# Second feed-forward, last eight tiles: the down projection by seven block products, with half of the weight sums made earlier on GpSimd

## The chip, the cores and the metric

The kernel runs on one core of one Trainium2 chip. Five engines share the work: TensorE (PE) multiplies matrices, VectorE (DVE) and ScalarE (ACT) do elementwise work and move results out of PSUM, GpSimd (POOL) does elementwise work in SBUF, and SyncE (SP) issues the transfers. The metric is the time of one execution on the device in microseconds (us), as the median of several runs.

## The reference

One layer on 512 latent tokens and 256 context tokens, all in float32, with model width 1024:

```python
def ffn_sublayer(h_in, shift, scale, gate, norm_w, w1, w3, w2):
    h = modulate(rms_norm(h_in, norm_w), shift, scale)
    return h_in + 0.5 * gate * swiglu(h, w1, w3, w2)      # swiglu: (silu(h @ w1) * (h @ w3)) @ w2
...
    x = ffn_sublayer(x, mx[0], mx[1], mx[2], norm1_w, ffn1_w1, ffn1_w3, ffn1_w2)
    ctx = ffn_sublayer(ctx, mc[0], mc[1], mc[2], norm1_w, ffn1_w1, ffn1_w3, ffn1_w2)
    proj = modulate(rms_norm(x, norm2_w), mx[3], mx[4]) @ w_in
...
    x = x + mx[5] * token_mix(proj, k_all, v_all, rope, ...)
...
    x = ffn_sublayer(x, mx[6], mx[7], mx[8], norm3_w, ffn2_w1, ffn2_w3, ffn2_w2)
    return x
```

`w1` and `w3` are 1024 x 2816 and `w2` is 2816 x 1024. The inner width 2816 is handled as 22 tiles of 128, `f` = 0 to 21. The first feed-forward runs on latent and context tokens, the second on the latent tokens alone. Only the latent stream is returned.

## The kernel before

**Precision.** A float32 product is made of three passes over operands that are split into a high and a low part: high x high, low x high, high x low (`mm3`). ScalarE casts the high part (`oph`) and VectorE subtracts it from the source for the low part (`opl`). In the trace these are `CAST oph<-raw` or `oph<-block`, and `TENSOR_TENSOR opl<-raw,oph` or `opl<-block,oph`.

**Up projections.** From f=4 on (the first four tiles are plain) both feed-forwards form `h @ w1` and `h @ w3` of a tile together by the seven-product scheme of Strassen and Winograd: halves of the model dimension, the two weight matrices, and two halves of the tokens are the 2x2 blocks. `Winograd.unit` (L938) issues seven products, named B11, T1, B21, T2, T3, T4 and B22 after their token-side block; in the second feed-forward each is 12 matmuls of 128x256. The weight side needs four sums of the four 512-column quarters of a weight block of 1 MB; `prep` and `wants` (L851, L861) have GpSimd make them (`s<-block`, three times `block<-...`), 128x512 each. VectorE combines the results out of PSUM and writes the gated tile as a split pair `gh`, `gl`.

**Down projection.** After some units, `down_flow` (L791) multiplies the finished tiles of a chunk with their rows of `w2`: 8 output tiles x n tiles x 3 passes of 128x512, each output tile added to `x` with the gate. `CHUNKS2 = [4, 4, 4, 4, 2, 4]` sets the chunks; the last of them, f=18 to 21, is done by `down` behind the units, with the output transfers in its evacuations (`ev3` L2298 and `ev_half`).

**What sets the order.** Instructions that go through the recording helper stand at L60 in the profile and keep the order in which they are written, on their engine. `Flow` (`slot`, L105) runs ahead of PE: it prepares operand pairs in the order of a list (`plan`, L894), five pairs ahead, up to nine during a down; `product` (L912) takes one pair each and lets the number shrink back by one per unit. Semaphore waits between engines follow from the data.

**End of the first feed-forward.** Its last chunk of six tiles (f=16 to 21) goes down in two halves of 384 tokens: `last_mm` (L1227) is called 16 times, 8 output tiles for group 0 and then 8 for group 1. `last_ev` (L1238) adds a result to `x` on VectorE and squares it on ScalarE; `SsqAcc` (L414) sums the squares on VectorE (`sqa`), and the total goes as a split pair `sqh`, `sql` through PE (`mm<-sql,ones`). `norm2` (L1244) then makes the normalised tokens of the group (`hf`, and the pair `hh`, `hl`). The normalisation of group 0 runs on VectorE beside the down part of group 1, and that of group 1 beside the input projection (`in_k`, L1317), in which the matmuls with `ones` stand at a fixed place. GpSimd has no work there.

Of the kernel before, what the change touches and what calls it, by code (L numbers as in the profile page):

```python
# [31 lines left out]
CHUNKS2 = [4, 4, 4, 4, 2, 4]  # L32
# [43 lines left out]
class Halves:  # L76
# [5 lines left out]
    def __getitem__(self, key):  # L82
        i = key[1].start // 512
        return self.tiles[i][:, key[1].start - 512 * i : key[1].stop - 512 * i]

# [96 lines left out]
def layer_kernel(ctx: ExitStack, tc: tile.TileContext, xT, wfirst, wst, wada, wuq, wkpe, cols, wrope, vnw, rope, out):  # L182
# [4 lines left out]
    const = ctx.enter_context(tc.tile_pool(name="const", bufs=1))  # L187
    raws = ctx.enter_context(tc.tile_pool(name="raws", bufs=RAWS))
# [636 lines left out]
    U_DN2 = U_UP2 + 44  # L825
# [13 lines left out]
    class Winograd:  # L839


        def __init__(self, pool, n, u0, blocks, g_tile, sl_bufs, s1_bufs, third=None, held=None):
            self.third, self.held = third, held
            self.sl_bufs, self.s1_bufs = sl_bufs, s1_bufs
            self.ready = (None,)
            self.pool, self.n, self.u0, self.blocks, self.g_tile = pool, n, u0, blocks, g_tile

        def tmp(self, name, n, bufs=1):
            return self.pool.tile([P, n], F32, tag=name, bufs=bufs, name=f"{name}_{nc.next_id()}")

        def prep(self, f, eng=None, early=False):  # L851
            r = st.block(wst, (self.u0 + 2 * f) // 2, self.third if f % 3 == 0 else None)
            q = [r[:, i * 512 : i * 512 + 512] for i in range(4)]
            s1 = self.tmp("s1", 512, self.s1_bufs)
            if f != self.held:
                (eng or nc.gpsimd).tensor_add(s1, q[2], q[3])
            if early:
                eng.tensor_sub(q[2], q[0], q[2])
            self.ready = f, q, s1, nc.gpsimd if early else eng or nc.gpsimd, early

        def wants(self, f):  # L861
            q, s1, eng = [], [], []
# [9 lines left out]

            def block_sums():
# [12 lines left out]
            def third():  # L886
                a = st.operand(q[1])
                eng[0].tensor_sub(q[1], q[1], q[0])
                return a
# [4 lines left out]
        def plan(self, flow, f0, downs, late=False):  # L894
# [4 lines left out]
            for f in range(f0, NF):  # L899
                nxt = self.wants(f + 1) if f + 1 < NF else None  # L900
                nx = nxt[:1] if nxt else ()
                if f == self.late:
                    flow.todo.extend((w[3], w[4], w[2]) + nx + (w[1],) + w[5:])
                elif nxt is None:
# [7 lines left out]
        def product(self, bank, blk, first, pend, step=None, cut=False):  # L912
# [4 lines left out]
            flow.slot(step or (lambda: None))  # L917
            prod(bank, a, self.blocks[blk], self.n, first, cut)
# [3 lines left out]
        def open(self, f, step, f0=None, splits=()):  # L922
# [12 lines left out]
            self.product(banks[0], "B11", True, evac(), step)  # L935
            return banks, p1

        def unit(self, f, hd, step):  # L938
# [10 lines left out]

            def ev_u2():  # L950
# [3 lines left out]
            def ev_u2z():  # L954
                v.tensor_add(u2, Y, p1)
                yield
                v.tensor_add(Z, Z, u2)

            def ev_u3():
                nc.scalar.copy(u3, W)  # L960
                v.tensor_add(u3, Z, u3)
                yield

            def ev_lo():
                v.tensor_add(W, W, u2)
# [4 lines left out]
            def ev_hi(seeded=False):  # L970
# [4 lines left out]
                v.tensor_mul(Z, Z, u3)  # L975
# [11 lines left out]
            if f == self.late or f + 1 == NF:  # L987
# [11 lines left out]
            seeded = f != self.late and f + 1 < NF  # L999
            if f + 1 < NF and nxt is None:  # L1000
                nxt = self.open(f + 1, None)
            self.product(banks[3], "T4", False, ev_lo(), lambda: step(f, 3))
            self.product(banks[2], "B22", False, ev_hi(seeded), cut=n > 256 and f in DOWN1)
            return nxt

        def run(self, flow, f0, after, step=lambda f, i: None, opening=None, splits=()):
# [3 lines left out]
            for f in range(f0, NF):  # L1010
                hd = self.unit(f, hd, step)
                after(self.flow, f)
            flow.slot()
            other_banks()

# [210 lines left out]

    def last_mm(g, dt, mid=lambda: None):  # L1227
        pt = mm()
# [65 lines left out]
    for dt in range(NK):  # L1294
# [14 lines left out]
        pt = last_mm(1, dt, lambda: next(hA) if dt == 1 else None)  # L1309
    fctx.close()  # L1310
# [836 lines left out]
    def g2_tile(f):  # L2147
        gt[f] = tuple(f2.tile([P, 512], F32R, tag=t, bufs=6, name=f"{t}_{nc.next_id()}") for t in ("gh", "gl"))
# [51 lines left out]
    def diffs(i, j, between):  # L2200
# [23 lines left out]
    def ends2(f):  # L2224
        return [ci for ci in range(len(CHUNKS2) - 1) if starts2[ci] + CHUNKS2[ci] == f]

# [45 lines left out]
    wino = Winograd(f2, 256, U_UP2, blocks, g2_tile, 2, 2, f2, NPLAIN2 + 1)  # L2272
# [25 lines left out]
    def ev3(pt, dt, g, gn):  # L2298
        evac_lat(pt, dt, 2)
        nc.sync.dma_start(two(out[:, dt, :]), lat(x, dt))  # L2300

    def ev_half(pt, dt, g, gn):
        evac_x(pt, dt, seg_of(g // 256)[:1], 2)
        o = slice(g // 256 * 384, g // 256 * 384 + 256)
        nc.sync.dma_start(out[:, dt, g : g + 256], x[:, dt, o])

# [5 lines left out]
    st.more = f2ctx.enter_context(tc.tile_pool(name="ops2", bufs=1)), MORE  # L2312
    wino.run(flow, NPLAIN2, after2, splits=splits)
# [106 lines left out]
```

## Time and profile before

| | |
|---|---|
| median of 3 runs | 1104.12 us (1104.03 to 1104.24) |
| the profiled execution | 1104.5 us |
| its span (first to last instruction) | 1102.5 us |
| first feed-forward's last down, group 0 and group 1 | about 490 to 516 and 516 to 541 us |
| second feed-forward's units (from f=4) and downs | about 797 to 1100 us |
| granted TensorE clock, mean | 1.00 |
| moved from and to HBM | 122.58 and 2.10 MB |

Times in the profile are microseconds, "busy" is the time in which an engine executed, and the share is that of the span. A row of the trace has start, duration, engine, line of the kernel, operation, result and inputs by name, and the shape; a bracket behind it gives the engine's idle time just before and what ended it. A row of a group has the count, the busy time and the mean of one in ns, and the idle time before such instructions. "PEld" is TensorE's weight load, which runs beside the matmuls.

### The profile page before, as it was taken

To read this page: it belongs to the slowest core of one execution; us is meant where nothing else is said; L and a number is where in the kernel's file an instruction comes from. 1 tells how busy PE (TensorE), PEld (TensorE's weight loads), DVE (VectorE), ACT (ScalarE), POOL (GpSimd) and SP (SyncE) were. 2 spreads that over 40 slices of the span, in tenths; PEclk is the share of its full clock that TensorE was granted. 3 is DMA by queue.
4 is the path that set the end of the run, shared out by engine and by line. 5 is a ranking of instruction groups with operands and counts; after the bars stand their busy time and mean duration, and the time that the engine had idled before them with its cause. 6 is when DMAs were issued, how large, how long until landed. Compare 5 with 4: busy or idle time off the path is not lost.

```text
span 1102.5 us, 19621 instructions
## 1 busy us (share of the span) xinstructions
PE 1097.5 (100%) x7610; PEld 1052.5 (95%) x7610; DVE 892.8 (81%) x1594; ACT 536.5 (49%) x1115; POOL 310.3 (28%) x269
## 2 busy tenths in 40 slices
PE   9999999999999999999999999999999999999998
PEld 7899999999999999999998889999999989898997
DVE  5779998888878769866867899989988878787883
ACT  6545422431344214443765549986663535354450
POOL 0003303311344013400009317860014444352420
PEclk9999999999999999999999999999999999999999
DMA  9721354234334664412241310103222322424202
GB/s 354 279 60 47 120 172 139 100 137 148 106 124 151 233 201 164 149 54 93 97 132 61 102 50 21 39 21 102 91 94 89 123 78 93 137 78 132 99 21 77
DMA packets 35677, 125.95 MB, mean 114 GB/s; under 512 B 3712, under 2 KB 10624, under 8 KB 30976
## 3 DMA queue, kind: packets, MB, share of 16 engines
q1 hardware_dynamic: 35440, 124.63, 33.2%
q8 instruction: 60, 0.98, 0.4%
q14 instruction: 33, 0.27, 0.1%
q10 hardware_dynamic: 144, 0.06, 0.1%
HBM read 122.58 MB, written 2.10 MB: 113 GB/s over the span
## 4 chain that ended last, share of the span: by engine, by line
PE 96%; DMA 1%; DVE 1%; ACT 1%; POOL 0%; issue 0%; SPq 0%; ACTq 0%; POOLq 0%; DVEq 0%
PE mm L60 61%; PE one L60 20%; PE big L60 10%; PE big L616 1%; PE mm L601 1%; DMA scale<-wada 1%; PE mm L177 1%; PE mm L176 1%; PE mm L178 1%; PE mm L338 1%; DMA x<-xT 0%; PE big L608 0%; DVE sq L60 0%; POOL pe L60 0%; ACT hh L60 0%
## 5 line engine op out<-in xcount | busy, mean ns | idle before, releaser
L60 DVE TENSOR_TENSOR opl<-block,oph 128x512 fp32r<-128x512 f32 x216 | 195.4, 912 | 32.6 <-ACT oph L60 29.9
L60 POOL TENSOR_TENSOR block<-block 128x512 f32<-128x512 f32 x69 | 105.0, 1522 | 378.9 <-DVE opl L60 376.2
L60 ACT CAST oph<-block 128x512 fp32r<-128x512 f32 x216 | 132.3, 622 | 108.8 <-PE mm L60 85.5
L60 PE MATMUL mm<-gl,oph 128*128 128x256 f32 (+2 forms) x573 | 176.4, 308 | 0.0
L60 PE MATMUL mm<-gh,opl 128*128 128x256 f32 (+2 forms) x573 | 176.4, 308 | 0.0
L60 PE MATMUL mm<-gh,oph 128*128 128x256 f32 (+2 forms) x573 | 176.4, 308 | 0.0
L60 PEld LDWEIGHTS mm<-gh,oph 128*128 128x128 f32 x573 | 107.6, 188 | 5.5
L60 PEld LDWEIGHTS mm<-gh,opl 128*128 128x128 f32 x573 | 107.6, 188 | 5.4
L60 PEld LDWEIGHTS mm<-gl,oph 128*128 128x128 f32 x573 | 107.6, 188 | 5.4
L60 ACT CAST oph<-raw 128x512 fp32r<-128x512 f32 x127 | 76.0, 620 | 69.7 <-PE mm L60 44.4
L60 DVE SCALAR_TENSOR_TENSOR x<-mm,g,x 128x512 f32<-128x512 f32 (+2 forms) x136 | 78.7, 600 | 28.5 <-PE mm L60 27.9
L60 DVE TENSOR_TENSOR opl<-raw,oph 128x512 fp32r<-128x512 f32 x127 | 88.1, 710 | 15.3 <-ACT oph L60 14.0
L60 POOL TENSOR_TENSOR block<-s,block 128x512 f32<-128x512 f32 x35 | 48.3, 1379 | 123.8 <-DVE opl L60 122.3
L60 PE MATMUL mm<-hh,oph 128*128 128x384 f32 (+2 forms) x195 | 64.9, 333 | 0.0
L60 PE MATMUL mm<-hl,oph 128*128 128x384 f32 (+2 forms) x195 | 64.8, 333 | 0.0
L60 PE MATMUL mm<-hh,opl 128*128 128x384 f32 (+2 forms) x195 | 64.8, 333 | 0.0
L60 DVE SCALAR_TENSOR_TENSOR junk<-raw,cb 128x1024 bf16<-128x1024 f32 x48 | 62.1, 1308 | 0.2 <-DMA raw<-wada 0.2
L60 POOL TENSOR_TENSOR s<-block 128x512 f32<-128x512 f32 x34 | 53.7, 1579 | 11.4 <-DMA block<-wst 11.4
L60 DVE SCALAR_TENSOR_TENSOR raw<-raw,cb 128x1024 f32<-128x1024 f32 x32 | 42.1, 1322 | 8.3 <-DMA raw<-wada 8.2
L60 PE MATMUL one<-hl,oph 128*128 128x384 f32 x144 | 48.1, 334 | 0.0
L60 PE MATMUL one<-hh,oph 128*128 128x384 f32 x144 | 48.1, 334 | 0.0
L60 PE MATMUL one<-hh,opl 128*128 128x384 f32 x144 | 48.1, 334 | 0.0
(699 smaller groups left out, 3361.9 us busy)
## 6 DMA issues: line engine op xcount, KB each, us to landing
raw<-wst SPq DMA_DIRECT2D x77, 512.0 KB, 3.8
block<-wst SPq DMA_DIRECT2D x36, 1024.0 KB, 4.9
raw<-wada SPq DMA_DIRECT2D x56, 512.0 KB, 4.3
scale<-wada SPq DMA_DIRECT2D x16, 512.0 KB, 9.0
x<-xT SPq DMA_DIRECT2D x5, 512.0 KB, 6.4
raw<-wfirst SPq DMA_DIRECT2D x8, 256.0 KB, 8.8
out<-x SPq DMA_DIRECT2D x7, 256.0 KB, 2.3
raw<-wuq SPq DMA_DIRECT2D x2, 384.0 KB, 5.1
```

Source lines behind the costliest of these rows:

```text
L60: return lambda *a, **k: self.tc.keep_in_program_order(f(*a, **k))
L176: nc.tensor.matmul(out, lh, rh, start=first, stop=False, skip_group_check=more)
L177: nc.tensor.matmul(out, lh, rl, start=False, stop=False, skip_group_check=more)
L178: nc.tensor.matmul(out, ll, rh, start=False, stop=last, skip_group_check=more)
L338: pin(nc.tensor.matmul(pa[q, :P], scw[:, kt, 2 - 2 * w : 34 - 2 * w], units[d][w][:, kt * P : kt * P + P], start=w == 0 and kt < 4, stop=w ...
L601: pin(nc.tensor.matmul(o, l[:, c], r, start=k == 0 and m == 0 and w == 0, stop=k == NK - 1 and m == 2, skip_group_check=True))
L616: pin(nc.tensor.matmul(two(pbs[i]), ops[k][lo][:, i * P : i * P + P], lat(r, k), start=False, stop=k == NK - 1 and m == 2, skip_group_chec ...
```

## The change

`CHUNKS2` becomes `[4, 4, 6]`: the downs behind units 4, 8 and 14 cover f=0 to 13. The last eight tiles go down together by four units of seven products (`unit7`), which continue the list of up units as f=22 to 25. In unit j the output tiles j and j+4, even and odd tiles f (two halves of the inner dimension, four tiles each), and two halves of 256 tokens are the 2x2 blocks. The token-side blocks are combined on VectorE and ScalarE while the up units of f=14 to 21 run (`Seven.combine`); every product is 12 matmuls of 128x256, and the results are added to `x` and sent out by `put`.

```diff
-CHUNKS2 = [4, 4, 4, 4, 2, 4]
+CHUNKS2 = [4, 4, 6]
+SEVEN2 = sum(CHUNKS2)
+SUMMED = 18
...
+        def unit7(self, f, hd):
...
+            x_part = (banks[0], blocks["B21"], False, ev_x())
+            self.product(banks[2], blocks["T1"], True, None)
+            last = f + 1 == self.end
+            if not last:
+                self.product(*x_part)
+            self.product(banks[1], blocks["T2"], True, ev_u2z())
+            self.product(banks[3], blocks["T3"], True, ev_w())
+            nxt = self.product(*x_part) if last else self.open(f + 1, None)
+            self.product(banks[3], blocks["T4"], False, ev_lo())
+            self.product(banks[2], blocks["B22"], False, ev_hi())
+            return nxt
...
+        def combine(self, f, W, Z, gh, gl):
...
+            if f % 2 == 0:
+                v.tensor_sub(t1, b12, W)
+                hi(gh, t1)
+                return [lambda: lo(gl, t1, gh)]
...
+            v.tensor_sub(t2, Z, t1)
+            hi(h[0], t2)
+            v.tensor_sub(t3, Z, b12)
...
+        def put(self, pt, dt, g, gate, whole=False):
+            o = x[:, dt, g * 384 : g * 384 + 256]
+            nc.vector.scalar_tensor_tensor(o, pt, gate[:, dt : dt + 1], o, ALU.mult, ALU.add)
+            if whole:
+                self.out(dt, g)
...
     nc.ordered = False
-    lastu = {}
-    last2 = (starts2[-1], CHUNKS2[-1], U_DN2 + starts2[-1])
-    down(*last2, [(0, 512)], ev3, range(NK - 1), lastu)
-    down(*last2, [(0, 256), (256, 256)], ev_half, range(NK - 1, NK), lastu)
```

The pairs still go through `Flow`; `plan` runs to f=25. Eight weight blocks of 1 MB, those of the up units f=18 to 21 and of the four new units, get their sums early: GpSimd makes them during the last down of the first feed-forward, in 16 half blocks with three buffers, and stores them in DRAM by SyncE. Each half is one load and one store of 512 KB and four additions of 128x256, done in place. Later the sums are loaded again beside three quarters of the block (`prep_sums`).

```diff
+    def presums():
...
+        def load(n):
+            staged[n] = stage.tile([P, 4, 256], F32, tag="quarters", name=f"quarters_{n}")
+            nc.sync.dma_start(staged[n], quarters(wst[U_UP2 // 2 + SUMMED + n // 2])[:, n % 2])
+
+        def store(n):
+            nc.sync.dma_start(quarters(block_sums[n // 2])[:, n % 2], staged.pop(n))
...
+        for n in range(m):
+            if n:
+                store(n - 1)
+            if n + 1 < m:
+                load(n + 1)
+            q = [staged[n][:, i, :] for i in range(4)]
+            for o, a in ((3, 2), (2, 0), (0, 3), (1, 0)):
+                nc.gpsimd.tensor_add(q[o], q[o], q[a])
+            yield
...
     def last_mm(g, dt, mid=lambda: None):
+        next(presum, None)
...
+        def prep_sums(self, f):
...
+            nc.sync.dma_start(a[:, 0:1024], src[:, 0:1024])
...
+            nc.sync.dma_start(t, block_sums[f - SUMMED])
+            nc.sync.dma_start(a[:, 1536:2048], src[:, 1536:2048])
```

So that the sums can be additions in place, the whole second feed-forward uses opposite signs on some weight sums, token differences and results:

```diff
-                    eng[0].tensor_sub(q[2], q[0], q[2])
-                eng[0].tensor_sub(q[0], s1[0], q[0])
+                    join(q[2], q[0], q[2])
+                join(q[0], s1[0], q[0])
...
-            nc.vector.tensor_sub(hA2, hA2, hB2)
+            nc.vector.tensor_sub(hA2, hB2, hA2)
```

Where the instructions stand is shown for three places. First GpSimd, from the sums of the last up unit of the first feed-forward (`block`) to the fill of a key tile (`kpT`) in the attention stage. Before:

```order
L60 TENSOR_TENSOR s_5851_5852<-block_5849 128x512
L60 TENSOR_TENSOR block_5849<-block_5849 128x512
L60 TENSOR_TENSOR block_5849<-s_5851_5852,block_5849 128x512
L60 TENSOR_TENSOR block_5849<-block_5849 128x512
L60 MEMSET kpT 64x768
```

And now, from the last of these sums:

```order
L62 TENSOR_TENSOR block_5859<-block_5859 128x512
L62 TENSOR_TENSOR quarters_6207<-quarters_6207 128x256 x4
L62 TENSOR_TENSOR quarters_6212<-quarters_6212 128x256 x4
L62 TENSOR_TENSOR quarters_6247<-quarters_6247 128x256 x4
L62 TENSOR_TENSOR quarters_6288<-quarters_6288 128x256 x4
```

The fill now stands behind sixteen such rows of four additions, of which the first four are shown.

Second SyncE's queue at the same time: the tables of the rotary embedding, then weights of the last down and of the input projection (`raw`). Before:

```order
L1194 DMA raw_6183<-wrope 128x64
L137 DMA raw_6251<-wst 128x1024
L137 DMA raw_6288<-wst 128x1024
L137 DMA raw_6323<-wst 128x1024
L137 DMA raw_6621<-wst 128x1024
```

Now (`quarters` is a half block, `sums` its place in DRAM):

```order
L1358 DMA raw_6193<-wrope 128x64
L1399 DMA quarters_6207<-wst 128x4x256
L1399 DMA quarters_6212<-wst 128x4x256
L1399 DMA quarters_6247<-wst 128x4x256
L149 DMA raw_6279<-wst 128x1024
L1402 DMA sums_60<-quarters_6207 512x1x256
L149 DMA raw_6323<-wst 128x1024
L1399 DMA quarters_6288<-wst 128x4x256
L1402 DMA sums_60<-quarters_6212 512x1x256
L149 DMA raw_6365<-wst 128x1024
```

Three loads go ahead of the first weight load; from then on loads, stores and weight loads alternate, and a load into a buffer stands behind the store that empties it.

Third VectorE at the end of an odd up unit late in the second feed-forward, between the low parts of two operands. Before:

```order
L60 TENSOR_TENSOR opl_13592<-raw_13587,oph_13590 128x512
L60 TENSOR_TENSOR one_13136<-one_13136,u_13418_13419 128x256
L60 TENSOR_TENSOR gl_13425<-one_13136,gh_13423 128x256
L60 TENSOR_TENSOR opl_13614<-raw_13587,oph_13612 128x512
L60 TENSOR_TENSOR opl_13636<-raw_13631,oph_13634 128x512
```

Now (`one` and `mm` are PSUM banks, `c` the scratch tiles of the combinations, `m0l` the low part of a combined block):

```order
L62 TENSOR_TENSOR opl_13298<-s_13221_13222,oph_13296 128x512
L62 TENSOR_TENSOR one_12766<-one_12766,u_13120_13121 128x256
L62 TENSOR_TENSOR c_10563<-one_12766,c_10561 128x256
L62 TENSOR_TENSOR c_10562<-one_12766,c_10562 128x256
L62 TENSOR_TENSOR m0l_10542<-c_10563,m0h_10541 128x256
L62 TENSOR_TENSOR c_10561<-c_10563,one_12764 128x256
L62 TENSOR_TENSOR opl_13324<-block_13219,oph_13322 128x512
L62 TENSOR_TENSOR m0l_10544<-c_10562,m0h_10543 128x256
```

Between the same two operand lows stand two combinations and more of 256 columns in place of one low part of `g`; further ones follow behind the next operand low.

More of the change, by code (lines that the diff above doesn't have):

```diff
@@ L849, in tmp, with wants_sums, first @@
             return self.pool.tile([P, n], F32, tag=name, bufs=bufs, name=f"{name}_{nc.next_id()}")
+        def prep_sums(self, f):
+            a = st.raw_pool.tile([P, 2048], F32, tag="block", bufs=BLOCKS, name=f"block_{nc.next_id()}")
+            src = wst[self.u0 // 2 + f]
+            nc.sync.dma_start(a[:, 0:1024], src[:, 0:1024])
+            pool = self.sums[f % 2]
+            t = pool.tile([P, 2048], F32, tag="block", bufs=1, name=f"s_{nc.next_id()}")
+            nc.sync.dma_start(t, block_sums[f - SUMMED])
+            nc.sync.dma_start(a[:, 1536:2048], src[:, 1536:2048])
+            q = [t_[:, j * 512 : j * 512 + 512] for t_, j in ((a, 0), (t, 3), (a, 1), (t, 0), (t, 2), (a, 3), (t, 1))]
+            self.ready = f, q
+        def wants_sums(self, f):
+            q = []
+            def first():
+                self.prep_sums(f)
+                q[:] = self.ready[1]
+                return st.operand(q[0])
+            return (first,) + tuple((lambda i=i: st.operand(q[i])) for i in range(1, 7))
         def prep(self, f, eng=None, early=False):
@@ L898, in plan @@
             flow.todo.append(w[0])
[L899 to L900 removed]
+            for f in range(f0, self.end):
+                nxt = self.wants(f + 1) if f + 1 < self.end else None
                 nx = nxt[:1] if nxt else ()
```

171 lines of the change are left out of this document (143 added, 28 removed).

## The prediction

> **What bounds the kernel now.** I read the page first, then TensorE's (PE's) waits, then its pace.
>
> ```profile
> span 1102.5 us, 19621 instructions
> PE 1097.5 (100%) x7610; PEld 1052.5 (95%) x7610; DVE 892.8 (81%) x1594; ACT 536.5 (49%) x1115; POOL 310.3 (28%) x269
> PE 96%; DMA 1%; DVE 1%; ACT 1%; POOL 0%; issue 0%; SPq 0%; ACTq 0%; POOLq 0%; DVEq 0%
> ```
> ```profile
> PE mm L296 <- DVE epsc L231: 1.0, 1, 1.0
> PE big L608 <- ACT hh L60: 0.4, 1, 0.4
> ```
>
> The chain that ended last is 96% PE, and the two largest of PE's waits are 1.0 and 0.4 us. So this kernel gets faster only if PE has less to do, and slower as soon as PE waits: there is no idle PE time in which a new wait could hide. VectorE (DVE) at 81% is the engine behind it. The profiled execution took 1104.5 us: 2.0 lie around the span, and it is 0.4 above the median of 1104.12.
>
> **What is removed and added on PE.** The next rows are starts within one down (512 columns a product) and within one up unit (256 columns).
>
> ```profile
> 1000.06 0.39 PE L60 MATMUL mm<-gh,opl 128*128 128x512 f32 x1
> ...
> 1019.10 0.39 PE L60 MATMUL mm<-gh,opl 128*128 128x512 f32 x1
> ```
> ```profile
> 1025.50 0.28 PE L60 MATMUL mm<-b11h,oph 128*128 128x256 f32 x1
> ...
> 1031.84 0.28 PE L60 MATMUL mm<-b21h,opl 128*128 128x256 f32 x1
> ```
>
> 84 steps in 19.04 us are 0.2267 us each; 56 steps in 6.34 us are 0.1132 us each. The eight tiles f=14..21 lose 8 output tiles x 8 f x 3 = 192 wide products, 43.5 us. The four new units bring 4 x 7 x 12 = 336 narrow ones, 38.0 us. **Net -5.5 us**, which counts in full, since PE sets the end. It is one eighth of those downs: seven block products for eight.
>
> The tail keeps its shape: a last product, one evacuation of 128x256, one transfer of 128 KB.
>
> ```profile
> 1099.16 0.28 PE L178 MATMUL mm<-gh,opl 128*128 128x256 f32 x1
> 1099.47 0.48 DVE L406 SCALAR_TENSOR_TENSOR x<-mm,g,x 128x256 f32<-128x256 f32 x1 [0.95 <-PE mm L178]
> out<-x SPq DMA_DIRECT2D x2, 128.0 KB, 1.7
> ```
>
> The other output transfers, now 16 of 128 KB, start during the last unit and are hidden by its products; I cost the tail at nothing. The flipped signs keep the number and size of instructions (a copy becomes a scaled copy, an addition a fused multiply and subtract), and the negated gate is one small multiplication in a stretch where PE runs on: nothing either.
>
> **The second feed-forward on DVE.** Two up units, the first with GpSimd (POOL) making sums, the second with none (columns: us, then busy time and count of PE, PEld, DVE, ACT, POOL, then granted clock, DMA share, GB/s):
>
> ```profile
> 919.30:928.80 9.50, 9.50 (x86) 9.50 (x85) 8.53 (x16) 5.16 (x12) 4.77 (x4) 1.00 0.32 113
> 1029.60:1039.10 9.50, 9.50 (x87) 9.50 (x85) 7.65 (x17) 5.18 (x13) 0.00 (x0) 1.00 0.58 203
> 914.09 1.80 POOL L60 TENSOR_TENSOR block<-block 128x512 f32<-128x512 f32 x1 [5.14 <-DVE opl L60]
> 914.65 0.42 DVE L60 TENSOR_TENSOR u<-mm,p 128x256 f32<-128x256 f32 x1
> ```
>
> From f=14 an even unit gains one DVE instruction of 256 columns and an odd one six. At 0.42 each, a pair of units costs 2 x 7.65 + 7 x 0.42 = 18.2 us of DVE, against 19.0 of PE. Where POOL still makes sums (to f=17) each unit costs 8.53 - 7.65 = 0.9 more, so units 15, 16 and 17 take 3 x 7.65 + 13 x 0.42 + 2.7 = 31.1 us of DVE against 28.5 of PE: 2.6 behind. The down after unit 14 leaves nine operand pairs ready; four of them, 12 x 0.1132 = 1.36 us each, are a lead of 5.4 us that covers it. Nothing, with rival D if it doesn't. ScalarE, at 5.2 of 9.5, has room for the casts that go with them. A unit whose sums are loaded needs 1.75 MB in 9.5 us, 184 GB/s, where the second row moved 203: nothing.
>
> The first new unit needs its third combination 3 x 1.36 + 1.0 = 5.1 us after the last up product. By then DVE has four operand lows (0.68 each, row below) and five operations of 0.42: 4.8. That leaves 0.3, less than one wait for ScalarE; I take **+0.3**, between 0 and one product of 1.36.
>
> **GpSimd at the end of the first feed-forward** decides the case. POOL was free there:
>
> ```profile
> 537.82 0.74 POOL L60 MEMSET kpT<- 64x768 f32 x1 [63.81 <-PE mm L60]
> 577.60 1.37 POOL L60 TENSOR_TENSOR rk<-vk,nhalf 128x6 f32<-128x6 f32 x1 [39.04 <-DVE vq L60]
> 483.85 0.42 SPq L1194 DMA_DIRECT2D raw<-wrope  x1
> raw<-wst SPq DMA_DIRECT2D x77, 512.0 KB, 3.8
> ```
>
> Now it gets 16 halves of four additions 128x256. The first load stands behind the transfer issued at 483.85, so additions begin at about 485 + 3.8 = 489. The fill at 537.82 then comes last on POOL, and the next work only 39 us later, so ending late costs POOL nothing. What such an addition does to DVE, the attention stage shows:
>
> ```profile
> 616.42 1.05 POOL L60 TENSOR_TENSOR ta<-qn,cosw 128x256 f32<-128x256 f32 x1 [3.43 <-DVE qn L60]
> 616.20 1.82 DVE L60 TENSOR_TENSOR opl<-raw,oph 128x512 fp32r<-128x512 f32 x2
> 569.97 1.28 DVE L60 TENSOR_TENSOR opl<-raw,oph 128x512 fp32r<-128x512 f32 x2
> 588.14 0.75 POOL L60 TENSOR_TENSOR qn<-ta,tb 128x256 f32<-128x256 f32 x1
> 588.18 1.25 DVE L60 TENSOR_TENSOR opl<-raw,oph 128x512 fp32r<-128x512 f32 x1 [0.58 <-ACT oph L60]
> ```
>
> Two operand lows take 1.28 alone and 1.82 with one POOL operation of 256 columns between them: 0.54 more. One low beside the other POOL row takes 1.25 instead of 0.64. The DVE instruction has two inputs in SBUF and lasts until POOL's is through. An instruction with one input in PSUM isn't held: the 0.42 row above began at 914.65, inside the POOL sum that ran from 914.09 to 915.89.
>
> The Trainium skill, "SBUF — State Buffer", section "Who interferes with whom", speaks against this change in the same way: a DVE instruction with two SBUF inputs and a GpSimd instruction that reads SBUF exclude each other for a whole instruction. The rows above agree (0.54 and 0.61). If every two-input operation below met an addition, that rule would give the upper bound of the sum, 11.2 us of waiting and 1110.4; by the mean over whole units (rival B) it would give none.
>
> What DVE does while PE runs the second half of that down, grouped (busy, mean ns, idle time before and its releaser):
>
> ```profile
> L60 DVE TENSOR_TENSOR hl<-hf,hh 128x384 fp32r<-128x384 f32 x8 | 4.4, 552 | 0.7 <-ACT hh L60 0.7
> L60 DVE TENSOR_TENSOR hf<-x,rstd 128x384 f32<-128x384 f32 x8 | 4.2, 551 | 0.1
> L60 DVE SCALAR_TENSOR_TENSOR x<-mm,g,x 128x256 f32<-128x256 f32 x8 | 3.8, 481 | 1.7 <-PE mm L60 1.6
> L60 DVE TENSOR_TENSOR sqa<-sqa,sq 128x384 f32<-128x384 f32 x6 | 3.3, 551 | 0.1
> L60 DVE TENSOR_TENSOR opl<-raw,oph 128x512 fp32r<-128x512 f32 x3 | 2.0, 682 | 0.0
> L60 DVE TENSOR_TENSOR sqa<-sq,sq 128x384 f32<-128x384 f32 x1 | 0.6, 559 | 0.6 <-ACT sq L60 0.6
> ```
> ```profile
> 541.00 0.56 DVE L60 TENSOR_TENSOR sql<-sqa,sqh 128x384 fp32r<-128x384 f32 x1 [0.58 <-ACT sqh L60]
> 543.01 0.33 PE L60 MATMUL mm<-sql,ones 128*128 128x384 f32 x1
> 557.98 0.56 DVE L60 TENSOR_TENSOR hl<-hf,hh 128x384 fp32r<-128x384 f32 x1 [0.87 <-ACT hh L60]
> 562.22 0.34 PE L60 MATMUL mm<-hh,oph 128*128 128x384 f32 x1
> ```
>
> Two-input operations: 8 + 8 + 6 + 3 + 1, and three single ones (sql, two steps of rstd): 29. Eight stand behind an evacuation of x, which reads PSUM and lets an addition pass. The other 21 can each meet one: 21 x 0.54 = 11.3. I take nine tenths, 10.2, since POOL pauses now and then for its transfers. A half in strict turns takes 4 x (0.54 + 0.56) = 4.4 us; with three buffers, (3.8 load + 4.4 additions + store) / 3 is 4.0 if a store takes as long as a load. No store of 512 KB stands in this trace (128 KB took 1.7), so POOL is close to either limit. Idle DVE time that can take it up is 0.7 + 1.7 + 0.6 = 3.0. PE executes in order, and its sum of squares at 543.01 has 543.01 - 541.56 = 1.45 in hand. So **10.2 - 3.0 - 1.45 = +5.75 us** of PE waiting, in bounds of 0 and 29 x 0.54 - 4.45 = 11.2. Behind that matmul the rest of the input projection is queued, so all of it moves.
>
> The same place of the first half:
>
> ```profile
> L60 DVE SCALAR_TENSOR_TENSOR x<-mm,g,x 128x256 f32<-128x256 f32 x8 | 3.8, 478 | 3.1 <-PE mm L60 3.1
> 515.14 0.56 DVE L60 TENSOR_TENSOR sql<-sqa,sqh 128x384 fp32r<-128x384 f32 x1 [0.58 <-ACT sqh L60]
> 516.29 0.33 PE L60 MATMUL mm<-sql,ones 128*128 128x384 f32 x1
> ```
>
> Here DVE has 3.1 us of idle time at the evacuations and fewer two-input operations, so only the last two before the matmul count: 2 x 0.54 against 516.29 - 515.70 = 0.59 in hand. That is 0.5 if both meet an addition; I take **+0.3**, between 0 and 1.
>
> Behind 541.5 the second normalisation has 21 more such operations up to 557.98 (8 hf, 8 hl, five others):
>
> ```profile
> L60 DVE TENSOR_TENSOR hl<-hf,hh 128x384 fp32r<-128x384 f32 x8 | 4.5, 559 | 3.8 <-ACT hh L60 3.8
> L60 DVE SCALAR_TENSOR_TENSOR rv<-mm,ri 128x384 f32<-128x384 f32 x1 | 0.6, 558 | 0.6 <-ACT ri L60 0.6
> ```
>
> It has 3.8 + 0.6 = 4.4 us idle there, and its last hl ends 562.22 - 558.54 = 3.7 before PE's use: 8.1 in all. At some 3.8 us a half before 516 and 4.4 after, 14 halves are done at the sum of squares, and two are left that end 9 us later; the 12 waits they can cause, 6.5 us, fit. Nothing.
>
> On SyncE's queue 16 loads and 16 stores of 512 KB come among the input projection's weight loads. A load waits there for a buffer that a store must leave, and a weight load behind it waits too; the weight loads run ahead of their use, so I cost it at nothing, and rival F prices it. In f=18..21 POOL loses 16 sums; PE didn't wait for them, so no gain.
>
> **Sum.** 1104.5 - 5.5 + 5.75 + 0.3 + 0.3 = 1105.4 on the profiled execution, less 0.4: **1105.0**.
>
> **Rivals.**
> A, the sum above: 1102 to 1106.8 as nine tenths become six tenths to all.
> B, *the waits disappear in DVE's own slack.* For it: in the two unit rows 4.77 us of POOL cost DVE only 0.88, or 0.18 per us. 25 us of additions would cost 4.5, just the 4.45 at hand. Against it: units have many PSUM operations, this stretch few. 1104.1 - 5.5 + 0.3 = 1099.
> C, slower: *POOL never pauses, and its additions outlast 558.* The point is about 4.7 us a half: (564 - 489) / 16, with the wait. Then the first place costs 11.3 - 4.45 = 6.9, the later chain 21 x 0.54 - 8.1 = 3.2, and 0.6 as before: 1109.3. For it: strict turns alone give 4.4, and a slow store adds to it.
> D, *DVE becomes the bound in f=14..21*, since no down lets it catch up: the 2.6 above on top of A: 1107.6. Against it: the lead of 5.4.
> E, *the clock after a wait.* The granted clock is 1.00 in both rows, and the longest PE wait 1.0; nothing here shows it after one of 5.75. Between nothing and half the wait again: 1107.5.
> The Trainium skill, "TensorE: Matmul & The Clock Gate", Part 1, would halve the clock after an idle window of about 3.4 us; by estimate another 2 to 3 us. No run here shows it.
> F, *the change doesn't do what it says*: products wait for sums or weights that come late, one half transfer (1.9) or so: 1107.
>
> **How the numbers follow.** A 0.39, B 0.33, C 0.15, D 0.06, E 0.04, F 0.03. About 0.2% (2.2 us) is what can be told from no change, so "same" is 1101.9 to 1106.3. B gives 0.31 faster and 0.02 same; A 0.04 faster, 0.33 same, 0.02 slower; the others are slower: 0.35, 0.35, 0.30. The range reaches from B's end without any wait (1098.6) to 1109.5, which leaves out nearly half of C. A's own range is 1102 to 1106.8.
>
> **What would show it.** After: 735 wide and 4053 narrow products at the same pace. A PE wait of 3 to 8 us for sql near 543, DVE's hf and hl at about 1.1 us instead of 0.55, and POOL busy some 65 us there prove A; no such wait proves B; a second wait for hl near 560 proves C; PE waits in f=15..21 prove D. I'm wrong if POOL's additions and DVE's don't hold each other, or if the four new units take over 38.5 us.

## The result and the profile after

| | before | changed |
|---|---|---|
| median | 1104.18 us (4 runs, 1104.03 to 1104.31) | 1116.07 us (4 runs, 1114.79 to 1117.97) |
| ratio to before | | 1.0109, 95% interval 1.0092 to 1.0127 |
| the profiled execution, its span | 1104.5, 1102.5 us | 1117.97, 1116.2 us |

The change makes the kernel 11.9 us slower. The profiled execution is the longest of the four, 1.9 above their median. Two executions further down that ran at a mean granted clock of 0.66 and 0.56 (1560 us of the kernel before, 1819 us of the run with the pairs side by side) are left out of every comparison. The page, read for the same parts as before:

```profile
span 1116.2 us, 20091 instructions
PE 1099.6 (99%) x7736; PEld 1057.6 (95%) x7736; DVE 917.5 (82%) x1641; ACT 548.3 (49%) x1144; POOL 347.1 (31%) x317
PEclk9999999999999999999889999999999999999999
PE 86%; DMA 6%; POOL 3%; DVE 3%; ACT 1%; issue 1%; SPq 0%; POOLq 0%; ACTq 0%; DVEq 0%
```

Some records of matmuls are missing, so PE's busy time isn't the place to look for the 5.5 us. Two things stand out. The chain that ended last now runs through DMA, POOL and DVE, and the granted clock (in tenths, 40 slices) falls to 8 in the slices from 530 to 586 us. The waits of TensorE show where:

```profile
PE big L62 <- DVE opl L62: 4.1, 2, 2.1
PE big L62 <- issue: 2.2, 1, 2.2
PE mm L62 <- ACT oph L62: 1.5, 1, 1.5
PE mm L62 <- ACT kpT L62: 1.1, 1, 1.1
PE mm L62 <- ACT sqh L62: 0.5, 1, 0.5
```

To date the losses, take the same matmul in both traces. PE's order is the same in both kernels up to 938 us of before, where a down begins that the changed kernel doesn't have. Before:

```profile
574.56 0.36 PE L60 MATMUL big<-ones,sqq 128*128 128x1 f32 x2
```

After, with the two matmuls on `sql`, which the prediction shows at 516.29 and 543.01:

```profile
517.67 0.45 PE L62 MATMUL mm<-sql,ones 128*128 128x384 f32 x1 [0.15 <-DVE sql L62]
551.44 0.34 PE L62 MATMUL mm<-sql,ones 128*128 128x384 f32 x1
590.20 0.36 PE L62 MATMUL big<-ones,sqq 128*128 128x1 f32 x2
```

PE is 1.4 us late at the first, 8.4 at the second, and 15.6 at the last: three losses of 1.4, 7.0 and 7.2. The span is 13.7 longer, so the rest of the kernel, mostly the second feed-forward, gives back about 2 and not 5.5.

The **first two losses** come from VectorE. Its groups between 516 and 550 us, and the same groups of before in their 25 us:

```profile
L62 DVE TENSOR_TENSOR hl<-hf,hh 128x384 fp32r<-128x384 f32 x8 | 8.2, 1021 | 0.7 <-ACT hh L62 0.7
L62 DVE TENSOR_TENSOR hf<-x,rstd 128x384 f32<-128x384 f32 x8 | 6.7, 863 | 0.1
L62 DVE SCALAR_TENSOR_TENSOR x<-mm,g,x 128x256 f32<-128x256 f32 x8 | 3.8, 475 | 0.0
```
```profile
L60 DVE TENSOR_TENSOR hl<-hf,hh 128x384 fp32r<-128x384 f32 x8 | 4.4, 552 | 0.7 <-ACT hh L60 0.7
L60 DVE TENSOR_TENSOR hf<-x,rstd 128x384 f32<-128x384 f32 x8 | 4.2, 551 | 0.1
```

The two-input instructions take 1.02 and 0.86 us in place of 0.55. The evacuation from PSUM keeps its 0.48, but its idle time, 1.7 before, is gone. The clock, in windows (columns as in the prediction):

```profile
538.00:542.00 4.00, 2.54 (x15) 2.18 (x13) 4.00 (x7) 2.21 (x5) 3.27 (x4) 1.00 0.85 254
542.00:546.00 4.00, 1.33 (x6) 1.03 (x7) 4.00 (x8) 0.60 (x2) 2.80 (x4) 0.68 0.97 305
546.00:550.00 4.00, 4.00 (x16) 3.90 (x15) 3.42 (x5) 2.05 (x5) 3.84 (x4) 0.50 0.64 243
580.00:585.00 5.00, 5.00 (x16) 4.00 (x15) 3.91 (x6) 3.19 (x6) 0.00 (x0) 0.56 0.28 85
```

DVE is busy 4.00 of 4.00 us where PE waits twice, 2.04 and 2.09 us with three matmuls (0.6 us) between. The granted clock falls during the second wait (0.68 in that window) and is 0.50 in the next window, in which PE doesn't wait any more. So of the 7.0 us, 4.1 are waits and the other 2.9 the clock behind them.

The **third loss** is another wait, here on ScalarE, on SyncE's queue and in the list of transfers (us from issue to landing):

```profile
572.95 0.47 ACT L62 COPY kpT<-mm 64x384 f32<-64x384 f32 x1 [5.56 <-DMA sums<-quarters]
```
```profile
558.44 11.75 SPq L1402 DMA_DIRECT2D sums<-quarters  x3
```
```profile
quarters<-wst SPq DMA_DIRECT2D x16, 512.0 KB, 5.6
sums<-quarters SPq DMA_DIRECT2D x16, 512.0 KB, 5.6
```

ScalarE stands 5.56 us before its copy to the key tile `kpT`, until the last store of the sums has landed. Behind it in its order are the operand casts that PE needs. PE waits 1.05 and 2.21 us and again gets half the clock (0.56 in the last window above): 3.3 of waits and 3.9 of clock.

### The profile page after: what moved, and what is told of

It reads as the page before. It is cut to its first block, busy times and chain, and to the rows that moved or that the text cites. A ratio compares the mean times of both kernels' runs of the same rounds, so it can differ in the third digit from the quotient of the medians.

```text
span 1116.2 us, 20091 instructions
## 1 busy us (share of the span) xinstructions
PE 1099.6 (99%) x7736; PEld 1057.6 (95%) x7736; DVE 917.5 (82%) x1641; ACT 548.3 (49%) x1144; POOL 347.1 (31%) x317
## 4 chain that ended last, share of the span: by engine, by line
PE 86%; DMA 6%; POOL 3%; DVE 3%; ACT 1%; issue 1%; SPq 0%; POOLq 0%; ACTq 0%; DVEq 0%
PE mm L62 54%; PE one L62 20%; PE big L62 9%; POOL quarters L62 3%; DMA quarters<-wst 2%; DMA sums<-quarters 2%; DVE opl L62 1%; PE big L630 1%; PE mm L615 1%; DMA scale<-wada 1%; PE mm L352 1%; ACT oph L62 0%; DMA x<-xT 0%; PE big L622 0%; DVE sq L62 0%
## 5 line engine op out<-in xcount | busy, mean ns | idle before, releaser
L62 DVE TENSOR_TENSOR opl<-block,oph 128x512 fp32r<-128x512 f32 x216 | 189.9, 887 | 27.5 <-ACT oph L62 24.8
L62 POOL TENSOR_TENSOR block<-block 128x512 f32<-128x512 f32 x61 | 93.4, 1531 | 345.6 <-DVE opl L62 338.5
L62 PE MATMUL mm<-gh,oph 128*128 128x256 f32 (+2 forms) x563 | 170.3, 303 | 0.0
L62 PE MATMUL mm<-gh,opl 128*128 128x256 f32 (+2 forms) x563 | 170.3, 303 | 0.0
L62 PE MATMUL mm<-gl,oph 128*128 128x256 f32 (+2 forms) x563 | 170.3, 302 | 0.0
L62 ACT CAST oph<-raw 128x512 fp32r<-128x512 f32 x119 | 70.9, 619 | 73.4 <-PE mm L62 44.9
L62 DVE SCALAR_TENSOR_TENSOR x<-mm,g,x 128x512 f32<-128x512 f32 (+1 forms) x124 | 69.0, 577 | 30.2 <-PE mm L62 29.9
L62 POOL TENSOR_TENSOR quarters<-quarters 128x256 f32<-128x256 f32 x64 | 58.3, 916 | 37.4 <-DMA quarters<-wst 33.5
L62 ACT CAST oph<-s 128x512 fp32r<-128x512 f32 x64 | 38.9, 621 | 37.6 <-PE mm L62 20.8
L62 POOL TENSOR_TENSOR s<-block 128x512 f32<-128x512 f32 x30 | 47.8, 1593 | 11.5 <-DMA block<-wst 11.5
```

What stands on the lines that cost most here:

```text
L62: return lambda *a, **k: self.tc.keep_in_program_order(f(*a, **k))
```

## Experiments

The theory after this reading: GpSimd's additions hold VectorE's two-input instructions (loss 1 and 2), the memory of the staging buffers holds `kpT` (loss 3), and the clock about doubles both. The rivals: the 16 MB of transfers delay the input projection's weights, or the new units themselves cost. Each run is compared with before, on the same chip.

**The seven products alone.**

```diff
-SUMMED = 18
+SUMMED = 26
```

> The seven-product down alone: no sums are made ahead, GpSimd makes those of all units f=14 to 25 during the second feed-forward, as before. Theory (the loss sits where the sums are made ahead): the 15.8 us that TensorE loses between 514 and 585 us of the span are gone, TensorE passes the rotary tables and the input projection at the times of before, and what is left is the second feed-forward's own result, which in the changed kernel was -1.3 us. VectorE gets 0.9 us more work in each of eight units, 4.6 behind by f=21 against a lead of 5.4, so some 0 to 3 us more: about 1104, 1102 to 1106. Rival (the new units are what costs): 1110 or more, with waits of TensorE behind 1070.

Measured: 1113.23 us (ratio 1.0081, 1.0065 to 1.0098). Half of each side came true. PE passes the end of the first feed-forward as before (0.2 us early at every matmul from 504 to 927), so the 15.6 us do belong to the sums made ahead. But the time is in the range of the rival, for a reason of neither. Its window behind 990 (columns as before) and, of the same stretch, the costliest group of VectorE:

```profile
990.00:1100.00 110.00, 101.00 (x851) 98.42 (x850) 101.77 (x176) 54.68 (x124) 55.06 (x36) 1.00 0.25 88
```
```profile
L62 DVE TENSOR_TENSOR opl<-block,oph 128x512 fp32r<-128x512 f32 x40 | 36.0, 919 | 1.4 <-ACT oph L62 0.8
```

Behind 990 GpSimd works 55 us, `opl` takes 0.92 us (0.73 in the run without these sums, below) and VectorE is busy 102 of 110. PE loses 9.0 in many waits of 0.3 to 1.5 us, and the clock stays 1.00. My 4.6 us behind against a lead of 5.4 was too little: the sums must not stand there either.

**The transfers without the additions.**

```diff
-            for o, a in ((3, 2), (2, 0), (0, 3), (1, 0)):
-                nc.gpsimd.tensor_add(q[o], q[o], q[a])
```

> The sums made ahead without their 64 additions: 16 loads and 16 stores stay, and the unsummed quarters are stored, so the weight sums of f=18 to 25 are left out. Theory (GpSimd's additions hold VectorE's two-input instructions): VectorE's hf, hl and sqa take 0.55 us again, no wait of TensorE at 516 and 540, and the granted clock stays 1.00; about 1102.8, 1101 to 1105. Rival (the transfers make the input projection's weights late, or hold the SBUF): the waits at 540 stay, 1108 or more. If the last store still ends behind 560, the second wait (for kpT) stays alone and the time is about 1107.

Measured: 1103.50 us (0.9994, 0.9985 to 1.0004), inside the theory's range. PE is 0.6 us late behind 516 and loses nothing more. Its wait list has no entry at 516, 540 or 575, and VectorE is as before:

```profile
L62 DVE TENSOR_TENSOR hl<-hf,hh 128x384 fp32r<-128x384 f32 x10 | 5.5, 554 | 1.6 <-ACT hh L62 1.6
```

So 16 MB more in 70 us cost this stage almost nothing, and the additions, with the late stores that follow from them, make the difference of 12.6 us.

**Half as many blocks.**

```diff
-SUMMED = 18
+SUMMED = 22
```

> Only the four new units' blocks are summed ahead (8 halves and 32 additions in place of 16 and 64); GpSimd makes those of f=18 to 21 in their units, as before. Theory (additions beside the normalisation, and a last store that a key tile waits for): the additions end near 530 us, so VectorE meets about half as many in the second half of the down, +1.5 to 3 us at 540 and +1.2 at 516, nothing behind 560; about 1106, 1103 to 1109. Rival (the stall is one event that any sums made ahead bring): 1112 or more.

Measured: 1116.95 us (1.0114, 1.0099 to 1.0129), a miss. The first part behaved: additions are through before the critical stretch, PE is 1.4 us late behind 516 and nothing is added up to 585. The second feed-forward lost the rest: one wait of 4.7 us and several of 0.6 to 1.3 between 1009 and 1079. The short ones stand where GpSimd makes the sums of f=18 to 21 again, as in the run of the seven products alone. The long one is a transfer (SyncE's queue and ScalarE):

```profile
1061.62 0.33 SPq L872 DMA_DIRECT2D s<-sums  x1
1066.43 0.62 ACT L62 CAST oph<-s 128x512 fp32r<-128x512 f32 x1 [5.56 <-DMA s<-sums]
```

A load of ready sums goes out at 1061.62 and lands 4.7 us later. ScalarE waits for it, and the evacuation that PE needs stands behind that cast. Why this load held PE here and not in the changed kernel stays open. I had looked at one end only.

**The key tile in memory of its own.**

```diff
+    p1bctx = ExitStack()
+    p1b = p1bctx.enter_context(tc.tile_pool(name="p1b", bufs=1))
...
-    kpT = p1a.tile([P, 768], F32, name="kpT")
+    kpT = p1b.tile([P, 768], F32, name="kpT")
```

> The changed kernel with the key tile kpT and four small tiles in a pool of their own, whose memory isn't the staging buffers': ScalarE's copy to kpT no longer waits for the last stores. Theory (the second loss, 7.2 us between 564 and 585, is that wait and the half clock behind it): 1116.1 - 7.2 = about 1109, 1107 to 1111. Rival (GpSimd's fill of kpT behind the last additions, or the weight load behind the last store on SyncE's queue, takes its place): 1113 to 1117.

Measured: 1110.34 us (1.0060, 1.0043 to 1.0076), as the theory says. All waits of PE between 480 and 640:

```profile
PE big L62 <- DVE opl L62: 2.6, 2, 1.5
PE mm L62 <- ACT sqh L62: 0.8, 1, 0.8
PE mm L62 <- DVE sql L62: 0.5, 1, 0.5
```

The wait for `kpT` is gone. In the built kernel the tile never overlapped the staging buffers (130144 to 133216 against 142720 and up, in bytes of a partition); its pool did. Here the memory was handed over as a whole pool: ScalarE's copy to `kpT` and GpSimd's fill of it both start when the last store out of the old pool has landed.

**GpSimd busy, but only writing**, first with fills of the same shape, then with fills as long as the additions.

```diff
-                nc.gpsimd.tensor_add(q[o], q[o], q[a])
+                nc.gpsimd.memset(q[o], 1.0)
```

> Each of the 64 additions becomes a fill of the same 128x256 (the sums of f=18 to 25 are left out): GpSimd is as busy, but reads nothing in SBUF. Theory (VectorE's two-input instructions are held only by a GpSimd instruction that reads SBUF): hf, hl and sqa take 0.55 us, no wait at 516 and 540, about 1103.5 as without additions. Rival (any GpSimd access holds them): hl at 1.0 us and more and the waits at 540 as in the changed kernel, 1109 or more.

Measured: 1103.97 us in one run. `hl` takes 0.553 us and nothing waits at 540, but a fill took only 0.31 us, so GpSimd was far less busy (17 us in place of 58). The next run repairs that:

```diff
+            for o in range(4):
+                nc.gpsimd.memset(staged[n], 1.0)
```

> The fills made as long as the additions: four fills of the whole 128x1024 half in place of four additions of 128x256 (the sums of f=18 to 25 are left out), since the fills of 128x256 took 0.27 us where an addition takes 0.75 alone. Theory (only a GpSimd instruction that reads SBUF holds VectorE): hf, hl and sqa stay at 0.55 us with GpSimd busy for some 60 us, no wait at 540, 1104 to 1106 (the last store still ends late, and kpT waits for it). Rival (GpSimd's writes hold VectorE too): hl near 1.0 us and the waits at 540, 1109 or more.

Measured: 1118.93 us in one run, far above the theory's 1104 to 1106, and the time alone misleads. GpSimd and VectorE, and all of PE's waits between 500 and 600:

```profile
L62 POOL MEMSET quarters<- 128x1024 f32 x64 | 60.7, 954 | 38.3 <-DMA quarters<-wst 35.5
L62 DVE TENSOR_TENSOR hl<-hf,hh 128x384 fp32r<-128x384 f32 x10 | 5.5, 554 | 1.6 <-ACT hh L62 1.6
```
```profile
PE mm L62 <- ACT kpT L62: 13.3, 1, 13.3
PE big L62 <- issue: 1.1, 1, 1.1
```

GpSimd is as busy as with the additions (60.7 us against 58.3, 0.95 a piece against 0.92), VectorE's instructions keep 0.55, and PE is on time to 0.04 us up to 558. So it is the reading that holds VectorE. The 1119 is the `kpT` wait and the clock behind it: PE is on time at 564, the last store lands at 576.7, and the wait is 13.3 us. In the changed kernel the last store lands earlier, at 572.9, so there PE on time would have waited some 9.5 us, an estimate from the two traces; the first losses had hidden most of that. So the losses don't add: taking away only the hold would have gained little.

**A pause in the critical stretch**: 6 halves beside group 0, none beside group 1, 10 behind it in the memory of `qn` and `ut`.

```diff
+    presum = presums(EARLY, 2 * len(block_sums), lambda n: spare[(n - EARLY) % 5])
```

> All sums ahead as in the change, but 6 halves during group 0 of the last down, none during group 1, and 10 behind it, during the input projection, with the memory of qn and ut as buffers. Theory (only additions between 516 and 545 cost, where VectorE's normalisation has little slack, and stores only where new tiles wait for them): the losses of 7.0 and 7.2 us go, at most 1.5 at 516 stays, and with -1.6 from the second feed-forward the time is 1103.5, 1102 to 1105.5. Rival (the second normalisation at 545 to 560 suffers as much, or qn waits for its stores behind 580): 1107 or more, with waits of TensorE there.

Measured: 1115.07 us (1.0095, 1.0078 to 1.0112): the rival. PE is 1.7 us late from 516 to 540 and 2.6 at 558, so the pause does what it should. Then GpSimd adds without a break from 544.6 to 583, and PE loses 2.7 more up to 577. The largest wait comes behind that:

```profile
PE big L63 <- DVE kpe L63: 5.4, 1, 5.4
```
```profile
580.25 0.52 SPq L1403 DMA_DIRECT2D sums<-ut  x1
580.86 1.46 SPq L150 DMA_DIRECT2D raw<-wst  x2
```
```profile
588.18 0.62 ACT L63 CAST oph<-raw 128x512 fp32r<-128x512 f32 x1 [3.05 <-DMA raw<-wst]
```

It doesn't come from `qn`: VectorE writes its first result there at 592.7 and waits for no store. A store of sums stands on SyncE's queue until GpSimd's additions are through at 580.24. The load of weights behind it goes out at 580.86 and lands at 588.1, and the cast of these weights, their low part and `kpe` follow in that order. That is 5.4 us and half clock behind it, 8.3 together.

**The pause, and two repairs of the new units**: `gh` and `gl` moved by 64 bytes, and an evacuation that the fifth product doesn't need put behind the one it does.

```diff
-    f2.tile([P, 16], F32, bufs=1, name="pad_f2")
+    f2.tile([P, 32], F32, bufs=1, name="pad_f2")
...
             def ev_w():
-                put(W, j + 4, 1, gate[1], True)
+                put(W, j + 4, 1, gate[1])
                 yield
+                put(Z, j + 4, 1, gate[1], True)
```

> The kernel with the pause, and in the second feed-forward the gh and gl tiles moved by 64 bytes and the evacuation that the fifth product doesn't need put behind the one it does. Theory (the new units' products run at 116 to 118 ns in place of 113.3 where they read gh and gl, by where these stand; and the first new unit's wait of 1.5 us is VectorE's queue ahead of that evacuation): 113.5 ns in these rows, -1.0 us, and the wait shorter by 0.5: 1102. Rival (the pace has nothing to do with where they stand): -0.5 alone.

Measured: 1118.87 us (1.0129, 1.0114 to 1.0144). The new evacuation order works: the first new unit's wait is 0.77 us in place of 1.50. The move brought nothing. The products on `gh` still step at 118 ns, and in the profiled execution those of the up units do as well, in part, through the whole second feed-forward: PE falls 2.4 us further back between 699 and 935. No other trace here shows that before 830 us, so the move is the likely cause, but it is one traced execution.

**No sums at all for f=18 to 25**: what the products are worth.

```diff
-            if f != self.held:
+            if f != self.held and not none:
```

> The seven-product down alone, with no weight sums of f=18 to 25 at all (left out, neither ahead nor in the units): what the products alone are worth. Theory (GpSimd's sums cost where they stand, the products save little more than a quarter of 5.5): TensorE at the end of the first feed-forward as before, FFN2 -1.6 us; against the same kernel with the sums in their units (1113.2) this is 10 to 11 us, all from VectorE waiting behind GpSimd: 1102.5, 1101.5 to 1104. Rival (the 9 us of that kernel come from VectorE's own new work): 1109 or more.

Measured: 1102.59 us (0.9990, 0.9981 to 0.9999). That is the ceiling of this change with GpSimd's work given away, and it comes in two sizes: seven of the eleven times lie at 1102.3 to 1102.7, -1.7 us, and four at 1104.0 to 1104.4, which is no gain. Its windows against those of the run with the sums in their units, above:

```profile
990.00:1097.00 107.00, 105.53 (x918) 105.18 (x917) 91.03 (x185) 55.21 (x125) 7.73 (x5) 1.00 0.27 95
```

GpSimd 8 us in place of 55, VectorE 91 of 107: VectorE's own new work fits, and the 10.6 us between the two runs are GpSimd's additions.

**The best placing I had**: 8 halves and 8, `qn` free earlier, and the evacuations reordered. Against the run with the pause:

```diff
-EARLY = 6
+EARLY = 8
```

> The best placing I have: 8 halves during group 0, 8 behind the down, with qn's memory free of them some 8 us earlier than with 6 and 10, and the new units' evacuations in the order that the fifth product needs. Theory: +1.7 at 516, +2 to 3 between 545 and 580 from VectorE's lower parts, nothing at qn, -2.3 in the second feed-forward: 1105.5, 1104 to 1108. Rival (GpSimd without pause behind 545 delays qn again): 1110 or more.

Measured: 1110.75 us (1.0059, 1.0047 to 1.0072): the rival again, in a smaller size. 0.8 us are lost at 516, 3.9 more up to 577, and PE waits 2.2 us at 584.6. Again it is a load of weights, as the chain that ended last shows:

```profile
576.35 8.03 DMA raw<-wst
```

No version that makes all its sums beat the kernel before.

**The pair of a tile side by side**, on the kernel without sums.

```diff
-            gt[f] = tuple(f2.tile([P, 512], F32R, tag=t, bufs=6, name=f"{t}_{nc.next_id()}") for t in ("gh", "gl"))
+            pair = f2.tile([P, 1024], F32R, tag="gh", bufs=6, name=f"gh_{nc.next_id()}")
+            gt[f] = pair[:, 0:512], pair[:, 512:1024]
```

> As the run without any sums of f=18 to 25, with gh and gl of a tile side by side in memory (2 KB apart, as those of f=14 are) in place of 12 KB apart. Theory (the distance of the pair makes the new units' products on gh and gl step at 118 ns): they step at 113.5 as those of f=14 do, -1.0 us against 1102.6. Rival (something else sets the pace): the same steps and the same time.

Measured: four times at 1102.3 to 1102.6 and five at 1103.9 to 1104.6 (ratio 0.9991, 0.9980 to 1.0001), about the same two sizes as without the pairs, so the medians say nothing here. The new units' products on `gh` and `gl` step at 118.5 ns where they stepped at 118.4. The pace has another cause, which stays open.

## Why the prediction was wrong

It forecast 1105.0, with an upper end of 1109.5, and the time is 1116.07. By its own steps:

- **Products, -5.5.** The trace has 735 wide products, as forecast, and 4067 narrow ones in place of 4053: the kernel before had split some products of these tiles, so 174 wide and 36 narrow ones went. At the forecast's own paces that is still -5.5. The pace is what failed. From the first product on f=14's gates to the last matmul there are 359 steps in 43.7 us. The first, the one that waited, and the last, in the order of time of PE:

```profile
1068.54 0.28 PE L62 MATMUL mm<-g14h,oph 128*128 128x256 f32 x1
...
1081.30 0.35 PE L62 MATMUL mm<-m0h,oph 128*128 128x256 f32 x1 [1.50 <-ACT oph L62]
...
1112.24 0.28 PE L62 MATMUL one<-t2h,opl 128*128 128x256 f32 x1
```

  Without the wait it is 42.0 us, 0.117 each in place of 0.1132. Over the 336 steps of the new units this term is mis-sized by +1.3. The trace of before could have told: the prediction took its pace from an up unit, but narrow products that read `gh` and `gl`, as some 140 of the 336 new ones do, stand at the end of that trace:

```profile
1096.40 0.28 PE L176 MATMUL mm<-gh,oph 128*128 128x256 f32 x1
...
1099.16 0.28 PE L178 MATMUL mm<-gh,opl 128*128 128x256 f32 x1
```

  These 23 steps take 2.76 us, 0.120 each.
- **First new unit, +0.3.** The wait is 1.5 us, inside neither the value nor the bound of 1.36. The reasoning went to the third combination; what is late is the evacuation queued behind it, as the two reordered versions show (0.77 and 0.91 us).
- **Tail, nothing.** From the start of the last matmul to the end it is 4.0 us in place of 3.3: +0.6. With these and a wait of 0.3 the sum for the second feed-forward is -1.8 and not -5.2; the changed kernel's trace gives -1.3.
- **Port wait, +5.75 and +0.3.** The mechanism is shown. Reading additions stretch VectorE's two-input instructions to 1.02 and 0.86 us, as the 0.54 for each predicts; long fills don't stretch them. The waits, 4.1 and about 0.7, are even a little below the term. They fall on `opl`, the input projection's operand just ahead of `sql` in VectorE's order, and not on `sql`. The Trainium skill, "SBUF — State Buffer", section "Who interferes with whom", names exactly this case, a GpSimd instruction that reads SBUF; these runs agree in both directions.
- **"Ending late costs POOL nothing"** is the step that failed worst, worth 7.2 here with the clock behind it (the key tile in memory of its own makes the kernel 5.7 faster). It followed GpSimd's next instruction and forgot the memory: the next pool was handed over only when the last store had landed. The store was also mis-timed, 5.6 us in place of 3.8, and a load too. So a half took (569.7 - 489.7) / 16 = 5.0 us from the first addition to the last, beyond the 4.7 from which rival C counts. C foresaw a late wait, but for `hl`.
- **The clock**, rival E with a chance of 0.04. The rows had only a longest wait of 1.0 us at a clock of 1.00. Here the clock is at half for 6.8 us twice, the first time behind (and during) two waits of 2.0 and 2.1 us, the second behind waits of 1.05 and 2.2:

```profile
540.07:543.48 3.41, 1.08 (x6) 0.67 (x5) 3.41 (x8) 1.30 (x3) 1.87 (x3) 1.00 0.83 245
543.48:550.30 6.82, 5.01 (x18) 4.82 (x19) 6.24 (x9) 2.68 (x6) 6.35 (x8) 0.50 0.83 287
577.61:584.44 6.83, 6.83 (x23) 5.96 (x24) 4.34 (x8) 4.69 (x10) 0.00 (x0) 0.50 0.46 175
```

  It costs 2.9 + 3.9 = 6.8 us in all. E and A weren't rivals: what makes E true is A's wait. They had to be added, not weighed.

Single waits show it too, in the run with half as many blocks. Its waits behind 1000, and the windows behind the longest:

```profile
PE one L62 <- ACT u L62: 4.7, 1, 4.7
```
```profile
1067.00:1069.00 2.00, 1.62 (x7) 1.62 (x8) 1.81 (x4) 2.00 (x6) 0.00 (x0) 0.58 0.02 4
1069.00:1071.00 2.00, 2.00 (x13) 2.00 (x12) 1.46 (x4) 0.15 (x1) 0.00 (x0) 0.57 0.00 0
1071.00:1073.00 2.00, 2.00 (x20) 2.00 (x19) 1.96 (x5) 1.17 (x3) 0.00 (x0) 1.00 0.00 0
```

That is 3.4 us at half the clock, and full speed again. The Trainium skill, "TensorE: Matmul & The Clock Gate", Part 1, puts the fall at an idle window of about 3.4 us. This wait agrees. In the changed kernel no single wait was that long: the two of 2.0 and 2.1 lie within 5 us with 0.6 us of work between them, so they agree only if the window is read as a share of time. In the run with the sums in their units, waits of up to 1.5 us, most of them 10 us or more apart, left the clock at 1.00. And the length of a wait alone doesn't decide: the 2.2 us of the best placing, from 584.55 to 586.80, left it at 1.00, too:

```profile
584.50:587.00 2.50, 0.25 (x2) 0.20 (x2) 2.07 (x7) 1.54 (x4) 1.04 (x1) 1.00 0.39 113
587.00:591.00 4.00, 4.00 (x21) 3.64 (x21) 3.51 (x10) 1.20 (x2) 3.97 (x7) 1.00 0.53 168
```

Between start and end of these kernels every stretch at half clock lasts 3.41 us or two or four times that. If the clock is set anew in steps of that length, which is an estimate from these stretches, PE was idle for 2.3 us of the step ahead of the first fall and for 2.2 ahead of the second, while the wait of the best placing is split by a step's end into 1.0 and 1.2 (counted in such steps from the rise of its clock at 5.3 us). Then the place of a wait counts as well as its length. What ends the half clock stays open: the last 3.4 us up to 584.4 are at half although PE doesn't wait in the step before.

The sum, on the profiled executions: +1.4 and +7.0 (hold and clock), +7.2 (memory and clock), -0.7 given back between 585 and 800, -1.3 in the second feed-forward, together 13.6 where 1117.97 - 1104.5 is 13.5. The profiled execution of the change is 1.9 above its median and that of before 0.3, so 1.6 go off for the medians: 11.9. The other executions weren't traced, so which of the losses were smaller in them isn't known.

## What to carry to other kernels

Work that is moved to an idle engine has four prices besides its own time: whom it holds while it reads, when its memory comes free for what is allocated next, what its stores do to that date, and which loads stand behind these stores. Ask for the last reader of the memory as well as for the next instruction. And when TensorE sets the end, price waits of some 2 us or more, and shorter ones that lie close together, at one to two times their length (2.2 us brought half the clock in one run here and not in another), and add that to the theory that brings them.

## What the runs showed of the hardware

- Products of 128x256 step at 113.3 ns or at about 118, over whole stretches, with the granted clock at 1.00. In one execution without the additions the units of f=18 to 21 all step at 117.8, in the changed kernel at 113.3; the repeated times of the kernel without sums lie at 1102.3 to 1102.7 and at 1104.0 to 1104.4. Neither 64 bytes of place nor the distance of the pair decided it for `gh` and `gl`; the cause is open.
- A fill on GpSimd, 128x1024 in 0.95 us, doesn't hold VectorE at all; additions of 128x256, 0.92 us each, stretch its two-input instructions from 0.55 to 0.86 and 1.02 us on average.
- Transfers of 512 KB took 5.6 us, loads and stores, where the columns of a half block come in pieces, and loads of whole rows 4.0 in the same kernel. In the run with long fills the same pieces took 4.5 and 4.8. The whole rows ran at other times, with less traffic beside them, so shape and traffic aren't told apart.
